# Second FFN of a recurrent decoder step: operands prepared in place and ahead, the last w_out block moved into the phase, the first part's outputs moved later

## The chip, the cores and the metric

The kernel runs on one core of a Trainium2 chip. The metric is device time in microseconds of one execution, and the median of three runs is given. A core has a matrix engine (TensorE, in the profile PE, with its weight loads as PEld), a vector engine (VectorE, DVE), a scalar engine (ScalarE, ACT), GpSimd (POOL) and SyncE (SP), which here issues nearly all DMA transfers, in order.

## The reference

One inference step of a one-layer hybrid decoder over 1104 tokens (16 learned tokens, 64 sample tokens, 1024 prompt tokens) of width 1024:

```
x = x + 0.5 * SwiGLU_1(RMSNorm(x))
x = x + W_out @ concat[RG-LRU, mLSTM, GLA](W_in @ RMSNorm(x))
x = x + 0.5 * SwiGLU_2(RMSNorm(x))
y = RMSNorm(x)                      # the final one
swiglu(x, w1, w3, w2) = (silu(x @ w1) * (x @ w3)) @ w2      # inner width 2816
```

All in float32; the states of the recurrences are outputs too.

## The kernel before

Activations lie transposed, 128 partitions of features by tokens. Every product of two float32 matrices is made of three matmuls in a rounded format: `split(hi, lo, x)` (L106) lets ScalarE cast x into hi, and VectorE subtract hi from x into lo; hi.hi + hi.lo + lo.hi are summed in a PSUM bank.

The program has three stages. The first FFN and the mixing work on three token blocks (336, 384, 384). In the mixing, nine chunks of recurrences are issued with a raised priority, and `w_out((0, 1), out01)` (L1032), the output projection of token blocks 0 and 1, fills TensorE between them. `w_out((2,), out01)` (L1035) follows for block 2: eight weight tiles of 512 KB, 24 matmuls of 384 columns for each, and a residual that is loaded, added and stored (`out01`, L987). The projection's inputs `ys[b]` are tiles named sh and sl in the pool `big`.

The second FFN (from L1267) has pools of its own, which lie where the earlier stages' tiles were. It works on two token parts (`PARTS`, L30): 576 tokens in two halves of 288, then 512 in two halves of 256. For each part `operands` (L1320) calls `norms` (L1291): eight squares on ScalarE, seven adds on POOL, sums over partitions by TensorE, a reciprocal root by eleven small VectorE operations (`rsq`, L110), and a broadcast by TensorE. Then it builds four normalised blocks b11, b12, b21, b22 (features by tokens, halved both ways), takes differences of them, and splits seven operands.

With these, a product of 2x2 blocks takes seven block products where eight would be usual (`seven`, L1388; 84 matmuls). A group f0 (two of 22 slices of 128 inner columns, so eleven groups) runs `seven` for w1 and for w3, the gates (L1490 to L1499), and the product with w2 (L1516 to L1527, called gemm2 here; 96 matmuls in part 0 and 48 wider ones in part 1), whose results VectorE adds into X[i]. The weights' own seven combinations are made by POOL (`weights`, L1360) and split into seven tiles. After the last group of part 0, five output blocks are transposed (`turned`, L1435), normed and stored (`output`, L1442). Part 1 ends with a special tail (L1482, L1500).

The framework orders the instructions of each engine by a priority, which is the order in which the program is written unless `high_priority` raises it, and by an estimate of when each is ready. Each engine then runs its list in order. It waits on a tile's buffer until the last user of that memory is done.

Of the kernel before, what the change touches and what calls it, by code (L numbers as in the profile page):

```python
# [7 lines left out]
F32 = mybir.dt.float32  # L8
# [3 lines left out]
OP = mybir.AluOpType  # L12
# [15 lines left out]
RB = 4  # L28

# [6 lines left out]
def tile_step(ctx, tc, A, O):  # L36
# [6 lines left out]
    wp = front.enter_context(tc.tile_pool(name="wp", bufs=3))  # L43
    mixing = ExitStack()
# [54 lines left out]
    def slot(i):  # L99
        return tuple(big.tile([128, 8, NB[i]], F32R, tag=f"{kind}{i}", name=f"{kind}{i}") for kind in ("sh", "sl"))  # L100
# [9 lines left out]
    def rsq(tp, v, p, n, tag=""):  # L110
        y = tp.tile([128, 4], F32, tag="rsy" + tag, name="rsy", bufs=RB)[:p, :n]
        a = tp.tile([128, 4], F32, tag="rsa" + tag, name="rsa", bufs=RB)[:p, :n]
# [158 lines left out]
    def mix(ph):  # L271
# [763 lines left out]
        w_out((2,), out01)  # L1035


    with ExitStack() as ph:
# [4 lines left out]
        park = [big.tile([128, 8, 384], F32R, tag=tag, name=tag) for tag in ("sl1", "sh2", "sl2")]  # L1043
# [223 lines left out]
    with ExitStack() as ph:  # L1267

        def pool(name, bufs=1, **kw):
            return ph.enter_context(tc.tile_pool(name=name, bufs=bufs, reuse_waits="tile", **kw))  # L1270

        xp, lp, op_, wq, tp = pool("x3"), pool("l3"), pool("o3"), pool("w3"), pool("t3", 2)
        pq, pz = pool("q3", 2, space=PSUM), pool("z3", 2, space=PSUM)
        psum["y"] = psum["s"] = psum["a"] = pz
# [7 lines left out]
        gb = xp.tile([128, 1024], F32, tag="gb", name="gb")  # L1282
        nc.sync.dma_start(gb, A["final_norm_g"].rearrange("(o d) -> o d", o=1).partition_broadcast(128))
        X = [xp.tile([128, 8, 2 * n], F32, tag=f"x{i}", name=f"x{i}") for i, (n, _) in enumerate(PARTS)]
        nc.sync.dma_start(X[0][:, :, 0:320], xdr2[0][:, :, 16:336])
        nc.sync.dma_start(X[0][:, :, 320:576], xdr2[1][:, :, 0:256])
        nc.sync.dma_start(X[1][:, :, 0:128], xdr2[1][:, :, 256:384])
        nc.sync.dma_start(X[1][:, :, 128:512], xdr2[2])


        def norms(i):  # L1291
            n = PARTS[i][0]
            r = tp.tile([128, 2, 288], F32, tag="rb", name="rb", bufs=1)[:, :, :n]
            acc = tp.tile([128, 576], F32, tag="h", name="acc", bufs=3)[:, : 2 * n]
            S.activation(acc, X[i][:, 0, :], AF.Square)
            for k in range(1, 8):
                q = tp.tile([128, 576], F32, tag="h", name="sq", bufs=3)[:, : 2 * n]
                S.activation(q, X[i][:, k, :], AF.Square)
                G.tensor_tensor(acc, acc, q, OP.add)  # L1299
            cs = [(o, min(128, n - o)) for o in range(0, n, 128)]  # L1300
            for h in range(2):
                ss = pz_("ssp")
                for j, (o, m) in enumerate(cs):
                    PE.matmul(ss[:m, j : j + 1], acc[:, h * n + o : h * n + o + m], ones[:, :1], start=True, stop=True)
                v = tp.tile([128, 4], F32, tag="rsv", name="rsv", bufs=RB)[:, : len(cs)]
                V.memset(v, 1.0)
                for j, (o, m) in enumerate(cs):
                    V.tensor_scalar(v[:m, j : j + 1], ss[:m, j : j + 1], 1.0 / D, EPS, OP.mult, OP.add)
                y = rsq(tp, v, 128, len(cs))
                q = pz_("rbp")  # L1310
                for j, (o, m) in enumerate(cs):
                    d = tp.tile([128, 128], F32, tag="dg", name="dg", bufs=3)
                    V.tensor_scalar(d[:m, :m], ident[:m, :m], y[:m, j : j + 1], None, OP.mult)
                    PE.matmul(q[:, o : o + m], ones[:m, :], d[:m, :m], start=True, stop=True)
                S.copy(r[:, h], q[:, :n])
            return r

        def operands(i, gname):  # L1320
            n = PARTS[i][0]
            r = norms(i)
            ops = {}
            for p in ORDER:
# [3 lines left out]
            def temp():  # L1328
                return lp.tile([128, 4, 288], F32, tag="bf", name="bf", bufs=4)[:, :, :n]

            def block(fh, th):
                t = temp()
                for k in range(4):
                    S.mul(t[:, k, :], X[i][:, 4 * fh + k, th * n : th * n + n], vc(gname, 4 * fh + k))
                V.tensor_tensor(t, t, r[:, th, None, :].to_broadcast([128, 4, n]), OP.mult)
                return t

            def minus(x, y, out=None):
                out = temp() if out is None else out
                V.tensor_tensor(out, x, y, OP.subtract)  # L1340
                return out

            b11, b12 = block(0, 0), block(0, 1)
            t1 = minus(b12, b11)
            split(*ops[1], b11)
            b22 = block(1, 1)
            t3 = minus(b22, b12, b12)
            t2 = minus(b22, t1)
            split(*ops[6], t2)
            b21 = block(1, 0)  # L1350
            split(*ops[2], b21)
            for p, t in ((7, t3), (5, t1)):
                split(*ops[p], t)
            split(*ops[4], minus(b21, t2, b21))
            split(*ops[3], b22)
            return ops
# [3 lines left out]
        def weights(w, f):  # L1360
            r = []
            for i in range(2):
                t = wq.tile([128, 4, 256], F32, tag="raw", name="wraw", bufs=3)
# [78 lines left out]
        def output(i, j, o, m, x, add=None):  # L1442
            ss = tp.tile([128, 2], F32, tag="ssf", name="ssf", bufs=RB)[:m]
            v = tp.tile([128, 4], F32, tag="rsv", name="rsv", bufs=RB)[:m, :1]
            for q in range(2):
                xq = x[:m, q * 512 : q * 512 + 512]
                if add:
                    add(q, xq)
                sq = tp.tile([128, 576], F32, tag="h", name="sqf", bufs=3)[:m, :512]
                S.activation(sq, xq, AF.Square, accum_out=ss[:, q : q + 1])  # L1450
                G.tensor_tensor(xq, xq, gb[:m, q * 512 : q * 512 + 512], OP.mult)
# [8 lines left out]
            for q in range(2):  # L1460
                h = slice(q * 512, q * 512 + 512)
                xq = x[:m, h]
                if q == 0:
# [3 lines left out]
                nc.sync.dma_start(dst[:, h], xq)  # L1467

        for i, (n, _) in enumerate(PARTS):
            ops = operands(i, "ffn2_norm_g")  # L1470
            for f0 in range(0, NFB, 2):
                last = f0 + 2 == NFB
                ys_ = {}
# [16 lines left out]
                for g in range(2):  # L1490
# [8 lines left out]
                    hs.append((hh, hl))  # L1499
                if tail:  # L1500
# [15 lines left out]
                for d in range(8):  # L1516
                    wh, wl = (t[:, :, d % 4 * 128 : d % 4 * 128 + 128] for t in u2[d // 4])
                    for o, m in ((0, n), (n, n)) if 2 * n > 512 else ((0, 2 * n),):
                        p = pz_("p2")
                        c = 0  # L1520
                        for g in range(2):
                            hh, hl = (t[:, o : o + m] for t in hs[g])
                            for w, x in ((wh, hh), (wh, hl), (wl, hh)):
                                PE.matmul(p[:, :m], w[:, g, :], x, start=c == 0, stop=c == 5)  # L1524
                                c += 1
                        xs = X[i][:, d, o : o + m]
                        V.scalar_tensor_tensor(xs, p[:, :m], 0.25, xs, OP.mult, OP.add)  # L1527
                if last:
                    for j, (o, m) in enumerate(PARTS[i][1]):
                        x = lp.tile([128, 1152], F32, tag="bf", name="xt", bufs=4)[:, :1024]  # L1530
                        turned(x, i, o, m)
                        output(i, j, o, m, x)
# [52 lines left out]
```

## Time and profile before

| | |
|---|---|
| median of three runs | 2263.55 us (2262.5 to 2268.26) |
| the profiled execution: time, span | 2263.99 us, 2262.2 us |
| mean granted clock of TensorE | 0.968 |
| PE busy, DVE busy, ACT busy, POOL busy | 94%, 68%, 38%, 16% of the span |
| second FFN | from about 1385 us to the end |

The span runs from the first to the last instruction; the time includes what lies around it. A stretch is two times in us from the span's start. The granted clock is a share of full speed: 1.00 is 2.4 GHz and 0.50 is 1.2 GHz. Matmuls overlap, so the time that one adds is found by dividing a stretch by their count.

### The profile page before, as it was taken

The page shows a single profiled execution, that of the slowest core. Times are in us where ns is not written, and L with a number is a line of the kernel's source. Part 1 is how long each engine was busy: PE and PEld are TensorE (multiplying, and loading weights), DVE is VectorE, ACT ScalarE, POOL GpSimd, SP SyncE. Part 2 cuts the span into 40 slices and gives each one's busy share as a digit, 9 for nine tenths or more (in the row PEclk, how much of TensorE's full clock was granted, in tenths as well). Part 3 has the DMA queues.
Part 4 walks back from the last instruction along what each step waited for, and adds up shares of the span by engine and source line. Part 5 has one row for each costly group of instructions (what it writes and reads, how often), then busy time and mean ns, then how long its engine had stood idle before and what let it go on. Part 6 is the DMA issues. An engine that isn't in the chain of part 4 may idle for free.

```text
span 2262.2 us, 35535 instructions
## 1 busy us (share of the span) xinstructions
PE 2118.2 (94%) x13758; PEld 2039.8 (90%) x13758; DVE 1532.1 (68%) x3207; ACT 865.6 (38%) x1701; POOL 371.4 (16%) x345
## 2 busy tenths in 40 slices
PE   8999999999999999999997995699999965999997
PEld 7999999999999999989987895699999955899996
DVE  6544445445444486665877862887888877888886
ACT  6211111111111155546556643443434344444443
POOL 3000000000000040000000002333333322434331
PEclk9999999999999999999998997699999986999999
DMA  5111111111111135434443356132333221333321
GB/s 176 34 51 38 47 38 47 47 38 55 30 56 48 38 112 138 140 115 130 114 123 83 84 149 201 54 94 85 94 94 94 85 74 44 103 94 112 103 94 47
DMA packets 237437, 192.50 MB, mean 85 GB/s; under 512 B 42079, under 2 KB 216708, under 8 KB 237012
## 3 DMA queue, kind: packets, MB, share of 16 engines
q1 hardware_dynamic: 232476, 188.45, 28.3%
q10 hardware_dynamic: 4792, 1.78, 0.4%
q8 instruction: 108, 1.77, 0.3%
q14 instruction: 61, 0.50, 0.1%
HBM read 159.40 MB, written 30.80 MB: 84 GB/s over the span
## 4 chain that ended last, share of the span: by engine, by line
PE 84%; DVE 8%; ACT 3%; DMA 3%; issue 1%; POOL 1%; SPq 0%; ACTq 0%; DVEq 0%; POOLq 0%
PE p L191 23%; PE p L1524 11%; PE p L240 11%; PE b L1397 9%; PE pw L191 8%; PE a L1397 6%; PE c L1397 5%; PE pwo L191 4%; PE pq L545 1%; DVE sl L129 1%; PE pA L747 1%; DVE wlo L108 1%; DVE rsa L116 1%; POOL acc L1299 1%; DVE rsy L118 1%
## 5 line engine op out<-in xcount | busy, mean ns | idle before, releaser
L107 ACT CAST whi<-wraw 128x512 fp32r<-128x512 f32 (+1 forms) x234 | 188.7, 806 | 345.0 <-PE p L240 116.4
L108 DVE TENSOR_TENSOR wlo<-wraw,whi 128x512 fp32r<-128x512 f32 (+1 forms) x234 | 244.7, 1046 | 19.7 <-ACT whi L107 16.9
L242 DVE SCALAR_TENSOR_TENSOR x<-p,x 128x384 f32<-128x384 f32 (+1 forms) x264 | 139.5, 539 | 154.1 <-PE p L240 153.6
L191 PE MATMUL p<-sh,whi 128*128 128x384 f32 (+1 forms) x1056 | 205.3, 332 | 0.4 <-ACT sh L128 0.4
L191 PE MATMUL p<-sl,whi 128*128 128x384 f32 (+1 forms) x1056 | 203.4, 330 | 0.0
L191 PE MATMUL p<-sh,wlo 128*128 128x384 f32 (+1 forms) x1056 | 202.1, 330 | 0.0
L1527 DVE SCALAR_TENSOR_TENSOR x<-p,x 128x288 f32<-128x288 f32 (+1 forms) x256 | 131.6, 526 | 76.2 <-PE p L1524 75.1
L191 PEld LDWEIGHTS p<-sh,whi 128*128 128x128 f32 x1056 | 179.7, 189 | 1.6 <-ACT sh L128 1.4
L191 PEld LDWEIGHTS p<-sh,wlo 128*128 128x128 f32 x1056 | 180.8, 188 | 0.0
L107 ACT CAST hh<-h 128x384 fp32r<-128x384 f32 (+3 forms) x110 | 61.4, 558 | 310.5 <-DVE h L224 278.3
L191 PEld LDWEIGHTS p<-sl,whi 128*128 128x128 f32 x1056 | 179.8, 188 | 0.1
L1372 POOL TENSOR_TENSOR ws<-wraw 128x512 f32<-128x512 f32 x88 | 136.1, 1546 | 258.3 <-DMA wraw<-in_ffn_w_dram 170.5
L240 PE MATMUL p<-hh,whi 128*128 128x384 f32 (+1 forms) x528 | 174.3, 330 | 1.9 <-DVE x L242 1.8
L240 PE MATMUL p<-hh,wlo 128*128 128x384 f32 (+1 forms) x528 | 174.2, 330 | 0.0
L240 PE MATMUL p<-hl,whi 128*128 128x384 f32 (+1 forms) x528 | 173.8, 329 | 0.0
L1397 PE MATMUL b<-op,whi 128*128 128x288 f32 (+1 forms) x1056 | 164.4, 293 | 6.4 <-ACT op L107 3.3
L107 ACT CAST whi<-ws 128x512 fp32r<-128x512 f32 x176 | 108.6, 620 | 160.7 <-PE b L1397 88.7
L1524 PE MATMUL p<-hl,w2h 128*128 128x288 f32 (+1 forms) x512 | 166.2, 326 | 2.2 <-DVE hl L108 2.2
L1524 PE MATMUL p<-hh,w2h 128*128 128x288 f32 (+1 forms) x512 | 163.2, 328 | 4.5 <-DVE x L1527 3.7
L1524 PE MATMUL p<-hh,w2l 128*128 128x288 f32 (+1 forms) x512 | 165.6, 325 | 0.0
L1397 PEld LDWEIGHTS b<-op,whi 128*128 128x128 f32 x1056 | 148.2, 192 | 10.6 <-ACT op L107 4.0
L143 POOL TENSOR_TENSOR acc<-acc,sq 128x384 f32<-128x384 f32 (+1 forms) x21 | 22.8, 1086 | 774.0 <-ACT sq L142 773.5
(455 smaller groups left out, 4619.6 us busy)
## 6 DMA issues: line engine op xcount, KB each, us to landing
wraw<-in_ffn_w_dram SPq DMA_DIRECT2D x154, 512.0 KB
w<-in_ffn_w_dram SPq DMA_DIRECT2D x44, 512.0 KB
wraw<-in_w_in_dram SPq DMA_DIRECT2D x16, 512.0 KB
wraw<-in_w_out_dram SPq DMA_DIRECT2D x16, 512.0 KB
out_y_prompt_dram<-xt SPq DMA_DIRECT2D x16, 256.0 KB
xspill<-x SPq DMA_DIRECT2D x2, 1536.0 KB
stg<-xspill SPq DMA_DIRECT2D x16, 192.0 KB
xspill<-stg SPq DMA_DIRECT2D x16, 192.0 KB
```

Source lines behind the costliest of these rows:

```text
L107: S.copy(hi, x)
L108: V.tensor_tensor(lo, x, hi.bitcast(F32), OP.subtract)
L116: V.tensor_tensor(a, y, y, OP.mult)
L118: V.scalar_tensor_tensor(y, a, 1.5, y, OP.add, OP.mult)
L143: G.tensor_tensor(sums[b], sums[b], s, OP.add)
L191: PE.matmul(p, wsl(ww, k), xsl(xx, k), start=i == 0, stop=i == tot - 1)
L240: PE.matmul(p[:, :n], w[:, g, :], x[:, :n], start=i == 0, stop=i == 3 * GRP - 1)
L242: V.scalar_tensor_tensor(X[b][:, d, :n], p[:, :n], 0.25, X[b][:, d, :n], OP.mult, OP.add)
L1372: G.tensor_tensor(t, x, y, op)
L1397: PE.matmul(t[:, :n], ww[:, k, :], xx[:, k, :], start=first and i == 0, stop=i == 11, skip_group_check=True,)
L1524: PE.matmul(p[:, :m], w[:, g, :], x, start=c == 0, stop=c == 5)
L1527: V.scalar_tensor_tensor(xs, p[:, :m], 0.25, xs, OP.mult, OP.add)
```

## The change

- Tiles sh2 and sl2 (the projection's input for block 2, and the first stage's parking place) move from `big` to a pool `yk` on the other side of the memory, which lives on into the second FFN.
- `w_out((2,))` goes from the end of the mixing to the second FFN as `wout2`, with a priority raised by 400, on weight tiles of the pool there (a fourth raw buffer is added), adding straight into X[1]. The residual for it is loaded from the first spill.
- `norms` adds on VectorE, not on POOL, and takes one root for both halves. `normal` multiplies X[i] in place by gain and root; `differences` and `operands` work on X[i] itself with two temporaries.
- X[0] is loaded again after its operands are split; X[1] is stored to `xback` and loaded again.
- norms(1) stands at group 4 of part 0, normal and differences at group 6; operands(1) in the last group, ahead of its gemm2.
- The outputs of part 0 follow group 2 of part 1, and their gain is multiplied on VectorE together with the root.
- The pool l3 (gates, w2 tiles, the final gain) is opened when `yk` is closed, and so lies on its place.

```diff
-        w_out((2,), out01)
...

+        pool = yk if i == 2 else big
...
-                G.tensor_tensor(acc, acc, q, OP.add)
+                V.tensor_tensor(acc, acc, q, OP.add)
...
+        def normal(i, r, ks):
+            n = PARTS[i][0]
+            for k in ks:
+                x = X[i][:, k, :].rearrange("p (h t) -> p h t", h=2)
+                V.scalar_tensor_tensor(x, x, vc("ffn2_norm_g", k), r, OP.mult, OP.mult)
...
+        def differences(i):
+            b11, b12, b21, b22 = blocks(i)
+            t1, t2 = temp(i), temp(i)
+            minus(t1, b12, b11)
+            minus(t2, b22, t1)
+            minus(b12, b22, b12)
+            return t1, t2
+
+        def operands(i, ts):
+            n = PARTS[i][0]
+            b11, t3, b21, b22 = blocks(i)
+            t1, t2 = ts
             ops = {}
+            for p, x in zip(ORDER, (b11, t2, b21, t3, t1, t2, b22)):
+                if p == 4:
+                    minus(t2, b21, t2)
                 t = op_.tile([128, 2, 4, 288], F32R, tag=f"op{p}", name=f"op{p}")
                 ops[p] = (t[:, 0, :, :n], t[:, 1, :, :n])
+                split(*ops[p], x)
             return ops
...
+        def wout2():
+            wo = A["w_out"].rearrange("(k p) f -> p k f", p=128)
+            for d in range(8):
+                raw = wq.tile([128, 4, 256], F32, tag="raw", name="wraw", bufs=4)
+                raw = raw.rearrange("p k f -> p (k f)").rearrange("p (k f) -> p k f", f=128)
+                nc.sync.dma_start(raw, wo[:, :, d * 128 : d * 128 + 128])
+                u = []
+                for c in range(2):
+                    hi = wq.tile([128, 4, 128], F32R, tag="whi", name="whi", bufs=7)
+                    lo = wq.tile([128, 4, 128], F32R, tag="wlo", name="wlo", bufs=7)
+                    split(hi, lo, raw[:, 4 * c : 4 * c + 4, :])
+                    u.append((hi, lo))
+                p = pz_("pwo")[:, :384]
+                i = 0
+                for a, b in ((0, 0), (0, 1), (1, 0)):
+                    for k in range(8):
+                        PE.matmul(p, u[k // 4][a][:, k % 4, :], ys[2][b][:, k, :], start=i == 0, stop=i == 23)
+                        i += 1
+                x = X[1][:, d, 128:512]
+                V.tensor_tensor(x, x, p, OP.add)
+
+        load0()
+        nc.sync.dma_start(X[1][:, :, 0:128], xdr2[1][:, :, 256:384])
+        nc.sync.dma_start(X[1][:, :, 128:512], xdr[2])
+        normal(0, norms(0), range(8))
+        ts = differences(0)
+        ops = operands(0, ts)
+        load0()
+        with tc.high_priority(offset=W2):
+            wout2()
+        late.close()
+        nc.sync.dma_start(xback, X[1])
+        lp = pool("l3")
...
+                if i == 0 and f0 == 4:
+                    r1 = norms(1)
+                if i == 0 and f0 == 6:
+                    normal(1, r1, range(8))
+                    ts = differences(1)
...
+                if i == 0 and last:
+                    ops = operands(1, ts)
+                    nc.sync.dma_start(X[1], xback)
...
+                gemm2(i, u2, hs)
+                if i == 1 and f0 == 2:
+                    outputs(0)
```

## Rows read from the trace of the kernel before

**Rows 1.** The page: busy time by engine; PE in 40 slices, tenths.

```profile
PE 2118.2 (94%) x13758; PEld 2039.8 (90%) x13758; DVE 1532.1 (68%) x3207; ACT 865.6 (38%) x1701; POOL 371.4 (16%) x345
...
PE   8999999999999999999997995699999965999997
```

**Rows 2.** Stretches: length, then busy time (and instructions) by engine, clock, DMA share, GB/s.

```profile
1385.50:1429.50 44.00, 4.13 (x18) 3.64 (x18) 20.41 (x43) 15.90 (x27) 21.97 (x15) 0.55 0.62 201
...
1429.50:1455.00 25.50, 18.01 (x75) 16.25 (x76) 21.28 (x22) 13.09 (x21) 2.87 (x2) 0.64 0.07 22
...
1455.00:1800.00 345.00, 344.99 (x2604) 344.53 (x2603) 290.98 (x471) 145.89 (x248) 131.65 (x86) 1.00 0.30 90
...
1800.00:1842.50 42.50, 35.76 (x240) 32.30 (x240) 29.63 (x54) 7.99 (x11) 1.28 (x1) 1.00 0.22 70
...
1842.50:1887.00 44.50, 9.71 (x51) 7.79 (x52) 31.61 (x102) 23.70 (x54) 21.45 (x17) 0.59 0.19 65
...
1887.00:1950.00 63.00, 54.78 (x362) 51.52 (x361) 57.81 (x76) 31.83 (x56) 22.23 (x14) 0.85 0.24 67
...
1950.00:2200.00 250.00, 250.00 (x1753) 233.70 (x1752) 214.51 (x324) 113.91 (x194) 94.86 (x65) 1.00 0.33 102
```

**Rows 3.** Waits of SP's queue, 1340 to 1440: total, times, longest.

```profile
SPq L1285 <- PE pwo L191: 2.7, 1, 2.7
```

**Rows 4.** Timeline of SP's issues: start, length, instruction.

```profile
1352.64 0.32 SPq L992 DMA_DIRECT2D xspill<-stg  x1
...
1385.46 0.53 SPq L1285 DMA_DIRECT2D x<-xspill  x1
```

**Rows 5.** Chain of waits through the first hole: start, length, what.

```profile
1348.18 3.39 DMA zg<-z_g
...
1352.75 32.70 PE pwo L191 x187
...
1386.74 8.56 DMA x<-xspill
...
1408.24 1.23 PE ssp L1304 x6
...
1422.29 1.20 DVE dg L1313
...
1429.48 1.37 DVE op L108
```

**Rows 6.** DMA in 1385 to 1400.

```profile
DMA packets 4185, 4.64 MB, mean 309 GB/s; under 512 B 94, under 2 KB 3906, under 8 KB 4185
```

**Rows 7.** Chain of waits through the second hole.

```profile
1870.49 0.72 ACT xt L1464
...
1886.25 1.22 PE a L1397 x4
```

**Rows 8.** VectorE's groups, 1354 to the end: count, busy us, mean ns, idle before.

```profile
L108 DVE TENSOR_TENSOR wlo<-ws,whi 128x512 fp32r<-128x512 f32 x176 | 143.9, 823 | 1.5 <-ACT whi L107 1.3
...
L1404 DVE TENSOR_TENSOR c<-p,b 128x288 f32<-128x288 f32 x66 | 29.5, 447 | 19.5 <-PE b L1397 18.9
...
L1494 DVE SCALAR_TENSOR_TENSOR h<-h,c 128x512 f32<-128x512 f32 x22 | 15.7, 743 | 0.2 <-ACT h L1493 0.2
...
L1340 DVE TENSOR_TENSOR bf<-bf 128x1152 f32<-128x1152 f32 x4 | 5.3, 1347 | 0.0
...
L1340 DVE TENSOR_TENSOR bf<-bf 128x1024 f32<-128x1024 f32 x4 | 4.8, 1218 | 0.0
```

**Rows 9.** Timeline of VectorE, root for half a part.

```profile
1878.55 0.22 DVE L1308 TENSOR_SCALAR rsv<-ssp 128x1 f32<-128x1 f32 x2 [7.51 <-PE ssp L1304]
...
1880.98 0.48 DVE L1313 TENSOR_SCALAR dg<-ident,rsy 128x128 f32<-128x128 f32 x2
```

**Rows 10.** Timeline of PE, eight transposes at the end of the kernel.

```profile
2229.77 1.04 PE L1439 MATMUL xps<-ident,x 128*128 128x128 f32 x8
```

**Rows 11.** Instructions on tile ws, 1500 to 1600: minimum, median, maximum ns.

```profile
L108 DVE TENSOR_TENSOR wlo<-ws,whi x24: 676/684/1476, 1500.5 to 1595.6; 128x512 fp32r<-128x512 f32 x24
```

More of the change, by code (lines that the diff above doesn't have):

```diff
@@ L43, in tile_step @@
     wp = front.enter_context(tc.tile_pool(name="wp", bufs=3))
+    late = ExitStack()
+    yk = late.enter_context(tc.tile_pool(name="yk", bufs=1, side="right"))
     mixing = ExitStack()
@@ L99, in slot @@
     def slot(i):
-        return tuple(big.tile([128, 8, NB[i]], F32R, tag=f"{kind}{i}", name=f"{kind}{i}") for kind in ("sh", "sl"))
+        pool = yk if i == 2 else big
+        return tuple(pool.tile([128, 8, NB[i]], F32R, tag=f"{kind}{i}", name=f"{kind}{i}") for kind in ("sh", "sl"))
     cols, cuts = list(NB), list(CHUNKS)
@@ L1042, in tile_step @@
         X = [xp.tile([128, 8, NB[b]], F32, tag=f"x{b}", name=f"x{b}") for b in range(3)]
-        park = [big.tile([128, 8, 384], F32R, tag=tag, name=tag) for tag in ("sl1", "sh2", "sl2")]
+        park = [p.tile([128, 8, 384], F32R, tag=tag, name=tag) for p, tag in ((big, "sl1"), (yk, "sh2"), (yk, "sl2"))]
         xt = {}
@@ new lines, in norms @@
+            cs = [(h, o, min(128, n - o)) for h in range(2) for o in range(0, n, 128)]
+            ss = pz_("ssp")
+            for j, (h, o, m) in enumerate(cs):
+                PE.matmul(ss[:m, j : j + 1], acc[:, h * n + o : h * n + o + m], ones[:, :1], start=True, stop=True)
+            v = tp.tile([128, 8], F32, tag="rsv", name="rsv", bufs=RB)[:, : len(cs)]
+            if n % 128:
+                V.memset(v, 1.0)
+                for j, (h, o, m) in enumerate(cs):
+                    V.tensor_scalar(v[:m, j : j + 1], ss[:m, j : j + 1], 1.0 / D, EPS, OP.mult, OP.add)
+            else:
+                V.tensor_scalar(v, ss[:, : len(cs)], 1.0 / D, EPS, OP.mult, OP.add)
@@ L1315, in norms @@
+            y = rsq(tp, v, 128, len(cs))
+            for h in range(2):
+                q = pz_("rbp")
+                for j, (hh, o, m) in enumerate(cs):
+                    if hh == h:
+                        d = tp.tile([128, 128], F32, tag="dg", name="dg", bufs=3)
+                        V.tensor_scalar(d[:m, :m], ident[:m, :m], y[:m, j : j + 1], None, OP.mult)
+                        PE.matmul(q[:, o : o + m], ones[:m, :], d[:m, :m], start=True, stop=True)
                 S.copy(r[:, h], q[:, :n])
@@ L1338, in minus @@
[L1338 to L1353, printed above, removed]
@@ L1442, in output @@
         def output(i, j, o, m, x, add=None):
+            ahead = add is not None
             ss = tp.tile([128, 2], F32, tag="ssf", name="ssf", bufs=RB)[:m]
-            v = tp.tile([128, 4], F32, tag="rsv", name="rsv", bufs=RB)[:m, :1]
+            v = tp.tile([128, 8], F32, tag="rsv", name="rsv", bufs=RB)[:m, :1]
             for q in range(2):
@@ L1462, in output @@
                 xq = x[:m, h]
-                if q == 0:
+                if not ahead:
+                    V.scalar_tensor_tensor(xq, xq, r, gb[:m, h], OP.mult, OP.mult)
+                elif q == 0:
                     S.mul(xq, xq, r)
@@ new lines, in tile_step @@
+        load0()
[10 more added lines that the diff above has]
+        lp = pool("l3")
+        gb = lp.tile([128, 1024], F32, tag="gb", name="gb")
+        nc.sync.dma_start(gb, A["final_norm_g"].rearrange("(o d) -> o d", o=1).partition_broadcast(128))
@@ new lines, in gemm2 @@
+        def gemm2(i, u2, hs):
+            n = PARTS[i][0]
+            for d in range(8):
+                wh, wl = (t[:, :, d % 4 * 128 : d % 4 * 128 + 128] for t in u2[d // 4])
+                for o, m in ((0, n), (n, n)) if 2 * n > 512 else ((0, 2 * n),):
+                    p = pz_("p2")
+                    c = 0
+                    for g in range(2):
+                        hh, hl = (t[:, o : o + m] for t in hs[g])
+                        for w, x in ((wh, hh), (wh, hl), (wl, hh)):
+                            PE.matmul(p[:, :m], w[:, g, :], x, start=c == 0, stop=c == 5)
+                            c += 1
+                    xs = X[i][:, d, o : o + m]
+                    V.scalar_tensor_tensor(xs, p[:, :m], 0.25, xs, OP.mult, OP.add)
@@ L1515, in tile_step @@
                     break
[L1516 to L1532, printed above, removed]
+                gemm2(i, u2, hs)
+                if i == 1 and f0 == 2:
+                    outputs(0)
 _INS = [
```

61 lines of the change are left out of this document (22 added, 39 removed).

## The prediction

> **What bounds the kernel now.** The page's head and its slices come first [rows 1]: TensorE (PE) is busy for 94% of the span, VectorE for 68%, and the PE slices drop below nine tenths in a shallow dip past the middle and in two deeper ones after it. So the kernel is TensorE-bound except in these two holes (the shallow dip, in the mixing, is not touched), and the change is about these. The table of stretches [rows 2] gives their size. Between the holes, from 1455 to 1800 us, 2604 matmuls take 345.0 us, 0.1325 us each, with TensorE never idle, the clock at its upper level (2.4 GHz) and VectorE at 84%. From 1950 to 2200 it is 1753 in 250.0 us, 0.1426 each, VectorE at 86%.
>
> The first hole: the last w_out block ends at 1385.4. By 1455 only 75 matmuls of the second FFN have been issued, which at 0.1325 is 9.9 us of work, so its first part runs as if it had started at 1445.1. Lost: 59.7 us. The second hole: in 1800 to 1842.5 there are 240 matmuls, 31.8 us of work, so 10.7 are lost. Then come 44.5 us with nearly none, and 362 matmuls from 1887 to 1950, 51.6 us of work at the later rate, so part 1 runs as if it had started at 1898.4; 55.9 lost. Together 66.6 us. In both holes the granted clock is 0.55 to 0.64, that is mostly the lower level (1.2 GHz); these counts contain that.
>
> Why the first hole is there is read from the chain of waits [rows 5] (the list names one step of each kind): w_out block (32.7 us of matmuls), load of X[0], eight squares and POOL adds, the sums over partitions, the reciprocal root, the diagonal, then one block at a time to the first split operand, which ends at 1430.9. The load itself waits for the last w_out matmul [rows 3] because X[0] lies where sh2 and sl2 were. Its data were there much earlier: the last store of token blocks 0 and 1 was issued at 1352.64, the load at 1385.46 [rows 4]. The second hole is the same chain, behind the five output blocks of part 0, which end at 1871.2; the first product of part 1 is at 1886.3 [rows 7].
>
> **The change, first hole.** It takes sh2 and sl2 off X[0]'s place, so the load can go at about 1352.6, 33 us earlier, and puts the w_out block on TensorE meanwhile. Step by step:
>
> The load was issued at 1385.46 and the first square started at 1395.33, after a stretch at 309 GB/s [rows 6]: 9.9 us. Now the eight w_out weight tiles (512 KB each) come on the same queue, and X[1] too. I add 3.5 us, for one such tile and a half ahead of it at that rate: squares start at 1366. Bounds are 0, if the scheduler puts X[0] first, and 14, if all eight tiles come first (4.2 MB at 309 GB/s).
>
> The w_out block now needs weight tiles of its own pool, which lie where the mixing's tiles were, so its first tile can't be fetched ahead. A small load in the chain is 3.4 us [rows 5] and a split of 128x512 is 0.7 on VectorE after a cast of about the same; I take 4.5 us later, ending at 1390. Bounds 0 and 8. Each of its eight products is 4.1 us of TensorE, over 2 splits and 1 add on VectorE, 1.9 us.
>
> Squares and adds: POOL's steps took from 1396.7 to 1408.2. On VectorE a two-input pass of 128x512 is 0.74 us where little disturbs it [rows 8]; for 128x576 I take 0.8. Seven of them and a square ahead are 6 us: 1372. Sums to diagonal took 14.1 us (1408.24 to 1422.29 [rows 5]), and 2.4 us for the same arithmetic with nothing between (1878.55 to 1880.98 [rows 9]); I take 7 with the sums' matmuls, since w_out's splits hold 1.9 of each 4.1 us: 1379. Broadcast and copies: 3.5. Eight in-place products of 0.8 and three differences of 1.35 [rows 8] are 10, and 13 with the rest of the w_out splits; cast and split of operand 1 are 2.5. First product: 1398.
>
> There TensorE is paced by VectorE for seven products: 7 operand splits of 1.35, 7 weight splits of 0.68 [rows 11] and 5 evictions of 0.45 [rows 8] are 16.5 us against 84 x 0.1325 = 11.1, so 5 lost, and I allow 2 for the lower clock after a gap of 8 us. Part 0 then runs as if started at 1405. **Saved in the first hole: 1445 - 1405 = 40 us.** Bounds: it can't start before the w_out block's end plus the 5, so at most 51; with the load 10 later still (its bound of 14), the w_out block 3.5 later and weights for the first products another 14 late behind all that, 12.
>
> The second load of X[0] waits on SP's queue for the last operand split, at about 1412, and the xback store for the last w_out add. Behind them on SP are the w2 tiles and the second weight set. The first FFN eviction that needs X[0] comes after two sets of 84 products, 22 us after the first; the reload is 2.36 MB, 7.6 us at 309 GB/s. I cost it at nothing, hidden by those products; without that cover it is 8 us, which lies inside those 14. The l3 tiles lie on sh2's place and so wait for the w_out block; it ends before the first product, so nothing.
>
> **The change, second hole.** What goes: the whole norm and block chain between the parts, and the output blocks, leave the hole. What stays at the seam: seven operand casts and splits (7 passes of 128x1024 at 1.2 us on VectorE [rows 8]), released one by one as the last products of part 0 free their tiles, beside the last gates (six passes, 4.4), 16 evictions of 0.45, the w2 splits (2.4) and seven weight splits of 0.68. All that is 27 us of VectorE against the gemm2 work left, which was 31.8 us in the trace [rows 2]. So it nearly hides; I leave 8 of the 66.6 us. If the gemm2 work is no longer left over there, the seam costs 15; if it hides fully, 0.
>
> What is added to the busy stretches. TensorE: 40 transposes of 0.13 us (eight in 1.04 us, [rows 10]) and eight small matmuls, 7 us with their PSUM turns. VectorE in part 0: 15 two-input passes of 128x512 (0.70), three differences of 1.2 and a root of 2.9: 17 us. In part 1: five blocks of two products (0.72) and 13 tiny operations (0.16): 18 us. The stretches have 15% of VectorE free, 5.3 us in each group of 35 us. The 17 fall on two groups and the 18 on about two, so 6 and 8 exceed what is free; weights are split one set ahead, and I charge half: 8 us with rounding up. POOL's adds and gain products of the first part go away and cost nothing, as POOL waits most of the time.
>
> Left in the second hole: 8 + 7 + 8 = 23. **Saved: 66.6 - 23 = 43.6.**
>
> Here a row and a rule meet. The same weight split of 128x512 takes 676 ns at least, 684 in the median and 1476 at most [rows 11], and 823 in the mean over the whole FFN [rows 8]; POOL's own passes run beside it. The Trainium skill, "SBUF — State Buffer", section "Who interferes with whom", says that a VectorE instruction with two SBUF inputs and a GpSimd instruction that reads SBUF exclude each other for the whole instruction, and so speaks against moving adds off POOL into a stretch where POOL still works. The spread of that row agrees. By the rule each moved pass costs its mean and not its minimum, and the sum would be that of the first rival below, 2216; by the median it is 2180.
>
> **Sum.** 2263.99 us (the profiled execution; its span is 2262.2) - 40 - 43.6 = 2180.4. The median of the runs shown is 0.4 lower, so 2180.
>
> **The rivals.**
> VectorE becomes the bound: its idle time in the busy stretches is waiting in step with TensorE and can't be used, so all moved work delays TensorE one for one: 17 + 18 + 8.4 us, times 823/684 = 52, and 7 of TensorE. The second hole then gives back 66.6 - 59 = 8. 2264 - 40 - 8 = 2216. For it: 84 to 86% in every stretch. Against it: TensorE never idled there. 14%.
>
> The w_out block hides nothing: X[0], the weights of w_out and those of the first products queue on one ring, and the first products start late. First hole 12 instead of 40: 2208. For it: 0.62 of all DMA time was already used there [rows 2]. 12%.
>
> Both hide better than I allow: 51 and 58: 2155. 8%.
>
> The preparation of part 1 doesn't run ahead: norms(1) needs tiles of the three "h" buffers that the gates use too, and slips to the seam; the 16 us from 1871 to 1887 stay: 2196. 5%.
>
> On the other side: the late outputs hold TensorE. Each block's transposes need one of two "bf" tiles, which comes free only when the store of the block before last has landed, and TensorE works in order. The five blocks took 29 us, 1842 to 1871, with all engines free for them. It costs more than the gain of 84 only from 17 us of held TensorE per block, three times that. 5%: 2% near no change, 3% slower, about 2290.
>
> The likeliest, 56%, is 2180, its own range 2166 to 2196. The range that leaves out no more than 2 in 10 takes in the two costly rivals: 2156 to 2216. A difference under 0.3% (7 us) can't be told from none here. Faster 0.95, same 0.02, slower 0.03.
>
> **What would show it.** First hole: the load of X[0] issued before the last w_out matmuls; no granted clock under 0.8 in a 25 us stretch from 1385 on; the first product near 1398. Second hole: no stretch of 25 us under 20 us of TensorE between the parts; the five output blocks spread inside part 1. VectorE at 0.9 over the second FFN. It would be wrong if TensorE showed new waits on weight splits in the groups that carry the moved work, on X[0]'s reload at the first evictions, or on transposes.

## The result and the profile after

The changed kernel takes 2229.08 us in the median (2227.4 to 2232.74, 4 runs) against 2263.03 for the kernel before, measured beside it: a ratio of 0.9848, 95% interval 0.9828 to 0.9868. It is faster by 34 us where 84 were forecast, and 13 us slower than the upper end of the range. The direction was right, the size was not.

The page of the changed kernel, its lines for TensorE, to be read beside [rows 1]: the matmuls are the same in number, and the shallow dip of the mixing is still there. The first deep hole (slices of 5 and 6) is now one slice of 4, further forward; of the second, two dents of 8 are left.

```profile
PE 2110.8 (95%) x13758; PEld 2035.0 (91%) x13758; DVE 1535.4 (69%) x3214; ACT 848.7 (38%) x1672; POOL 330.6 (15%) x321
...
PE   8999999999999999999998894999999989889997
```

The table of stretches, with the columns of [rows 2]:

```profile
1349.60:1386.40 36.80, 5.83 (x25) 5.05 (x24) 14.50 (x40) 9.67 (x16) 0.00 (x0) 0.56 0.80 226
1386.40:1425.00 38.60, 36.28 (x204) 35.54 (x204) 35.80 (x41) 18.06 (x25) 8.61 (x6) 0.97 0.51 168
1425.00:1775.00 350.00, 338.53 (x2525) 335.99 (x2525) 299.60 (x481) 146.09 (x252) 124.08 (x86) 1.00 0.31 96
1775.00:1850.00 75.00, 67.66 (x506) 66.95 (x505) 65.59 (x102) 32.25 (x51) 25.77 (x15) 0.93 0.34 111
1850.00:1925.00 75.00, 71.63 (x520) 68.34 (x520) 58.24 (x94) 29.49 (x51) 22.06 (x17) 0.98 0.29 92
1925.00:1975.00 50.00, 34.68 (x201) 29.96 (x200) 37.44 (x108) 23.58 (x51) 6.19 (x5) 0.83 0.27 90
1975.00:2180.00 205.00, 204.65 (x1431) 190.93 (x1430) 183.70 (x270) 91.16 (x157) 72.27 (x50) 1.00 0.30 96
```

Three things are to be seen. There is still a hole of 37 us, now ahead of the w_out block (clock 0.56). The body of part 0, where TensorE lost nothing before, now loses: 2525 matmuls in 350 us. And the five late output blocks leave a dent at 1925 to 1975.

By 1500 us the products of the second FFN count 564 in the changed kernel (450 with w1 and w3, 114 of gemm2) and 405 in the one before (345 and 60; rows below). At the 0.1325 us of one, part 0 runs as if started at 1425.3 against 1446.3: **21 us came from the first hole, where 40 were forecast.** The profiled executions differ by 35.3 us (2263.99 and 2228.67), so **14.3 came from the second, where 43.6 were forecast**: of its 66.6 us, 52.3 are still lost somewhere, not 23. Such splits by count hold to some 3 us: the w_out block begins at 1386.45 here, and at 1384.10 and 1383.17 in two runs below that differ from this kernel only behind it.

Products with w1 and w3 and of gemm2 from 1350 on, in the changed kernel and then in the one before (stretch, TensorE's time and count, clock, DMA share, GB/s):

```profile
1350.00:1500.00 150.00, 62.43 (x450) 0.89 0.54 166
...
1350.00:1500.00 150.00, 17.89 (x114) 0.89 0.54 166
```

```profile
1350.00:1500.00 150.00, 54.77 (x345) 0.81 0.39 122
...
1350.00:1500.00 150.00, 8.93 (x60) 0.81 0.39 122
```

### The profile page after: what moved, and what is told of

It is laid out like the page before. It is cut to its first block, busy times and chain, and to the rows that moved or that the text cites. A ratio compares the mean times of both kernels' runs of the same rounds, so it can differ in the third digit from the quotient of the medians.

```text
span 2226.9 us, 35462 instructions
## 1 busy us (share of the span) xinstructions
PE 2110.8 (95%) x13758; PEld 2035.0 (91%) x13758; DVE 1535.4 (69%) x3214; ACT 848.7 (38%) x1672; POOL 330.6 (15%) x321
## 4 chain that ended last, share of the span: by engine, by line
PE 83%; DVE 9%; ACT 3%; DMA 2%; issue 2%; SPq 1%; DVEq 0%; ACTq 0%
PE p L196 24%; PE p L245 11%; PE p L1528 10%; PE pw L196 10%; PE b L1405 8%; PE c L1405 5%; PE a L1405 5%; PE pwo L196 2%; DVE wlo L113 1%; PE pq L550 1%; PE pwo L1498 1%; PE pA L752 1%; DVE sl L134 1%; PE pgt L464 0%; DVE hl L113 0%
## 5 line engine op out<-in xcount | busy, mean ns | idle before, releaser
L113 DVE TENSOR_TENSOR wlo<-ws,whi 128x512 fp32r<-128x512 f32 x176 | 136.5, 779 | 5.2 <-ACT whi L112 4.1
```

Of the source, the lines that this page charges most:

```text
L113: V.tensor_tensor(lo, x, hi.bitcast(F32), OP.subtract)
```

## Experiments on the first hole

TensorE's longest wait of the changed kernel between 1345 and 1450 (total, times, longest), and its timeline there (start, length, instruction, and in brackets the wait before it and what ended it):

```profile
PE ssp L1307 <- DVE acc L1303: 27.9, 1, 27.9
```

```profile
1377.61 2.31 PE L1307 MATMUL ssp<-ones,acc 128*128 128x1 f32 x12 [27.86 <-DVE acc L1303]
1383.02 3.50 PE L1322 MATMUL rbp<-dg,ones 128*128 128x128 f32 x12 [3.10 <-DVE dg L1321]
1386.45 2.58 PE L1498 MATMUL pwo<-sh,whi 128*128 128x384 f32 x8
...
1411.14 1.22 PE L1405 MATMUL a<-op,whi 128*128 128x288 f32 x8
...
1423.30 1.55 PE L1498 MATMUL pwo<-sh,wlo 128*128 128x384 f32 x8
```

ScalarE cast the first w_out weights at 1361.81 (row below), so the first product could have run near 1363. It stood behind the norm's sums, which waited 27.9 us for the squares.

```profile
1361.81 1.14 ACT L112 CAST whi<-wraw 128x512 fp32r<-128x512 f32 x2 [12.26 <-DMA wraw<-in_w_out_dram]
```

What holds that order? Not the priority: with W2 at 2500 instead of 400 the instruction lists of all engines come out identical. The sums (ssp), the broadcasts (rbp) and the w_out products (pwo) share two PSUM banks, which are handed out in the order of the text, and there the norm stands first.

**Own banks for w_out.**

```diff
-                p = pz_("pwo")[:, :384]
+                p = bank("ac"[d % 2])[:, :384]
```

> The eight w_out products take their PSUM tile from two of the six banks of the products a and c, which nothing uses yet, instead of the two banks that they shared with the norm's sums (ssp) and broadcasts (rbp). Theory 1 (the shared banks): in the changed kernel the first w_out product has to take its bank after rbp, so it stood behind the whole norm on TensorE though its first weights were split by 1363.7. With banks of its own the block starts near 1364 and ends near 1400, and the sums stand behind it; the chain from sums to first operand (root, eight products, differences, splits: about 20 us) then starts at 1400, so the first product comes near 1420 instead of 1411 and the part starts as if at 1420 instead of 1424: 0 to 8 us faster, 2221 to 2229, with the hole not gone but moved behind the block. Rival (loads): X[0], X[1] and the w_out weights come late on one ring, whatever the order; the block then still starts after 1380 and the time stays within 3 us of 2229.

Measured 2223.63 (ratio 0.9821, 95% interval 0.9806 to 0.9835, which overlaps that of the changed kernel a little). Its timeline:

```profile
1359.69 2.93 PE L1498 MATMUL a<-sh,whi 128*128 128x384 f32 x8 [12.87 <-ACT whi L112]
...
1394.10 1.55 PE L1498 MATMUL c<-sh,wlo 128*128 128x384 f32 x8
1395.49 1.34 PE L1307 MATMUL ssp<-ones,acc 128*128 128x1 f32 x12
...
1408.87 1.33 PE L1405 MATMUL a<-op,whi 128*128 128x288 f32 x4 [4.71 <-ACT op L112]
```

One line moved the whole block 27 us forward, so the shared banks were the cause and the loads were not. But the sums now wait behind the block, and part 0 runs as if started at 1417.7 (621 products by 1500).

**The norm between the products.** Two ways: the block cut by hand into three pieces, still on the shared banks (first; the third piece stands behind the norm), and own banks with the norm at a higher priority (second).

```diff
+            if i == 0:
+                wout2(range(0, 3))
             ss = pz_("ssp")
...
             y = rsq(tp, v, 128, len(cs))
+            if i == 0:
+                wout2(range(3, 5))
...
+        wout2(range(5, 8))
...
-        with tc.high_priority(offset=W2):
-            wout2()
```

> The w_out block is written in three pieces inside the norm of part 0: three products ahead of the sums over partitions, two ahead of the broadcasts, three behind. Theory 1 (the shared banks and TensorE's order set by them): products run while ACT and VectorE do the squares and the root, the block ends near 1400, the first product of the FFN near 1405; effective start 1405 to 1410 instead of 1424, 14 to 19 us faster: 2210 to 2215. Rival (loads late): the pieces wait for weights, not for banks; under 5 us, 2224 to 2229. Rival (VectorE): the w_out splits and adds go in front of the norm's adds on VectorE, and the norm's end is as late as before: 5 to 10 us.

```diff
-        normal(0, norms(0), range(8))
+        with tc.high_priority(offset=2500):
+            r0 = norms(0)
+        normal(0, r0, range(8))
```

> As the kernel with own banks for the w_out products, and the norm of part 0 written with a higher priority, so that TensorE's list has the sums after the fifth product and the broadcasts after the seventh, with everything else in the same order. Theory 1 (TensorE's order, set by the shared banks): in the run with own banks the sums stood ready at 1378.6 and waited until 1395.5 behind the block; now the root and the products run beside the last three w_out products, the block ends near 1398 and the first product follows at once, near 1400 instead of 1409: 7 to 12 us faster than that run, 2211 to 2217. Rival (VectorE is what counts from 1395 on: in that run it was busy for 23 of 25 us from 1400 and for 25 of 25 from 1425): the operand splits and the first weight splits fill it whenever they start, and only 1 to 4 us are won, 2219 to 2223.

The first took 2234.32 (0.9871, 0.9854 to 0.9887), no gain over the changed kernel: without the priority the w_out loads stand behind those of X[0] and X[1], and TensorE waited 20.9 us for its first weights, until 1368.63. The second took 2220.07 (0.9811, 0.9793 to 0.9828), which the intervals do not tell from own banks alone. There the sums ran at 1383, the broadcasts at 1394 and 1398, and the first product came at 1403.86, 5 us earlier; yet by 1500 it has 619 products and starts as if at 1418.0. The table of stretches says why (the columns are those of [rows 2]):

```profile
1400.00:1450.00 50.00, 38.14 (x252) 35.75 (x251) 50.00 (x57) 25.67 (x40) 32.76 (x10) 0.90 0.52 174
```

VectorE is busy for 50.00 of 50 us: eight products, differences, seven operand splits and the first weight sets fill it whenever they start. The rival that named VectorE from 1395 on had the better forecast. Not all of these 50 us are work, though: from 1424.85 on, ten of VectorE's passes took 0.6 to 1.1 us longer than others of their shape, some 9 us together, while POOL's own passes ran (rows in the last section).

## Experiments on the second hole

**Leaving the two moved parts out.** One kernel drops the call of outputs(0). The other drops norms(1), normal(1) and differences(1) and sets the two temporaries to zero.

> Leaves out the five output blocks of part 0 (their rows of the output are not written). Measures what the late outputs cost. Theory (late outputs hold TensorE for about as long as in the hole that they left): 15 to 22 us faster, 2207 to 2214. Rival (they are hidden, TensorE pays the 40 transposes alone): 5 to 8 us faster, 2221 to 2224, and the waits at 1936 to 1959 turn up as something else.

> Leaves out the sums, the normalising products and the differences of part 1 (part 1 then runs on tokens that are not normalised, with zeros for two of its operands). Measures what the work ahead costs inside part 0. Theory (VectorE pays one for one in lost TensorE time): the 17.6 us that part 0 lost between 1425 and 1775 come back, 14 to 20 us faster, 2209 to 2215. Rival (the order of VectorE's list and its bursts, whatever work is in it: a wait of 2.3 us on an eviction at 1600 is after all of that work): under 8 us faster, 2221 to 2229.

Measured 2205.97 (0.9739, 0.9724 to 0.9753) and 2205.41 (0.9740, 0.9726 to 0.9755): the late outputs cost 23.1 us, the work ahead for part 1 costs 23.7, each give or take a few us. If the two add, about 5.5 of the 52.3 us are left for the seam itself, where 8 were forecast.

The stretch 1525 to 1775, in the changed kernel, then without the work ahead, then with that work paced (next run):

```profile
1525.00:1775.00 250.00, 239.75 (x1784) 237.69 (x1783) 207.14 (x341) 98.89 (x169) 79.21 (x57) 0.99 0.28 86
```

```profile
1525.00:1775.00 250.00, 250.00 (x1890) 249.80 (x1890) 214.74 (x340) 108.35 (x182) 83.55 (x58) 1.00 0.31 91
```

```profile
1525.00:1775.00 250.00, 245.59 (x1844) 243.95 (x1844) 216.55 (x355) 104.60 (x178) 81.47 (x58) 1.00 0.30 89
```

106 matmuls, 14.0 us, are lost to the work ahead in this stretch. But VectorE is *busier* in the kernel that loses nothing (214.74) than in the one that does (207.14): its total is not the bound. Nor is the loss where the passes are. In the changed kernel VectorE's products for part 1 run from 1552.6 to 1559 and the three differences end at 1568.6, but the 25 us from 1550 lose 8 matmuls, and later ones 30 and 20 (changed kernel; without the work ahead these three have 191, 190 and 191):

```profile
1550.00:1575.00 25.00, 24.44 (x183) 23.97 (x182) 25.00 (x34) 9.18 (x17) 9.38 (x7) 1.00 0.18 55
...
1600.00:1625.00 25.00, 22.68 (x160) 22.44 (x159) 19.16 (x33) 7.14 (x12) 6.26 (x5) 0.93 0.24 78
...
1700.00:1725.00 25.00, 22.89 (x171) 22.46 (x170) 19.46 (x34) 9.14 (x16) 7.64 (x5) 1.00 0.29 85
```

**Pacing the products.** In VectorE's list the eight products stand in one run (one and seven). Written into four groups they still come out in one run, since they are ready; so each pair is made to wait for its group's result. The differences follow the last pair, at group 14.

```diff
+                if pace:
+                    V.scalar_tensor_tensor(r1[:, :, 0:1], t[1][:, 0:2].rearrange(...), 0.0, r1[:, :, 0:1], OP.mult, OP.add)
+                    normal(1, r1, range(f0 - 6, f0 - 4))
```

> The same work ahead for part 1, but its eight products go two by two into four groups: each pair is made to wait for the group's first-FFN result (a product with zero of one column is added to the factors, one tiny operation per pair). Leaving the work out won 24 us, 14 of them between 1525 and 1775. Theory 2 (bursts: eight passes in a row stand ahead of evictions in VectorE's list, not the sum of the work; VectorE was 0.83 busy there, and 0.86 without any loss in the run without the work): half of the 14 or more comes back, 2217 to 2224. Rival (the sum of the work, one for one): 2226 to 2232.

Measured 2222.62 (0.9821, 0.9804 to 0.9838, overlapping that of the changed kernel a little): 6.5 us back in the medians, and 60 of the 106 matmuls, 8.0 us, in that stretch, with more passes than before. So more than half of the loss there came from the products' standing in one run and from where they stood, not from their sum. The waits of the changed kernel from 1560 to 1775 are for evictions that came late, nearly all of them after the last of these passes; how the run makes later evictions late is not shown:

```profile
PE b L1405 <- DVE c L1412: 5.0, 4, 2.1
PE p L1528 <- DVE x L1531: 2.3, 1, 2.3
PE c L1405 <- DVE c L1412: 1.7, 1, 1.7
```

The 2.3 us are followed by a lower clock, 0.93 in the slice of 25 us: single matmuls start 0.24 us apart instead of 0.13.

```profile
1600.10 0.29 PE L1528 MATMUL p<-hh,w2l 128*128 128x288 f32 x1
1602.72 0.40 PE L1528 MATMUL p<-hh,w2h 128*128 128x288 f32 x1 [2.32 <-DVE x L1531]
...
1603.66 0.45 PE L1528 MATMUL p<-hh,w2h 128*128 128x288 f32 x1
1603.90 0.45 PE L1528 MATMUL p<-hl,w2h 128*128 128x288 f32 x1
```

**The adds of part 1 back on POOL** (`(V if i == 0 else G).tensor_tensor(acc, acc, q, OP.add)`).

> The seven adds of part 1's sum of squares go back to POOL; seven passes of 0.7 us less on VectorE. Theory 2 (bursts; the adds stood one by one between other work in VectorE's list): 0 to 3 us faster, 2226 to 2229. Rival (the sum of the work, one for one, 24 us for about 20 of passes): 5 to 7 us faster, 2222 to 2224. Rival (the passes of POOL slow those of VectorE): slower than 2229.

Measured 2226.50 (0.9842, 0.9822 to 0.9863). The interval is nearly that of the changed kernel: whether seven passes less on VectorE are worth nothing or their sum of 4.8 us (seven of 0.68) can't be told from it.

**The output blocks: one to a group, one to every second group, back where they were, and with a third tile.**

```diff
-                if i == 1 and f0 == 2:
-                    outputs(0)
+                if i == 1 and 2 <= f0 <= 10:                    # one to a group
+                    outputs(0, [f0 // 2 - 1])
+                if i == 1 and f0 % 4 == 2 and f0 <= 18:         # every second group
+                    outputs(0, [f0 // 4])
+                if i == 0 and last:                             # back
+                    outputs(0)
...
-        ... pool("t3", 2), pool("b3", 2)
+        ... pool("t3", 2), pool("b3", 3)                        # third tile
```

> The five output blocks of part 0 one in each of five groups of part 1 instead of all behind the second group. In the changed kernel TensorE's list has all 40 transposes in one row, 8 and 32, and without the blocks the kernel took 23 us less. Theory 3 (TensorE is held because the blocks queue for two tiles, two PSUM banks and the stores among themselves): spread, only the 5 us of transposes and a little clock remain, 12 to 18 us faster, 2211 to 2217. Rival (each block costs its 4 to 5 us wherever it stands, by its work on VectorE): within 4 us of 2229.

> The five output blocks one in every second group of part 1. One to a group won 9.6 of the 23 us that they cost; 5.2 are transposes. Theory 3b (each block costs its own share wherever it stands, by its work on ACT and VectorE and by its transposes): as one to a group, 2217 to 2221. Rival (two blocks in neighbouring groups still meet at the tiles and the stores): 4 us or more faster than one to a group, 2215 or less.

> The output blocks of part 0 go back to where they were, right behind part 0, with all else as changed. In the kernel before they took 29 us there, with TensorE idle; now the operands of part 1 are ready and its products can run beside them. If the late place saved what the prediction took (their time in the hole, 29 us, against 7 of transposes and a part of 18 of VectorE): 10 us or more slower than 2229. Theory 3 (what costs is that all 40 transposes stand in one row of TensorE's list, wherever): within 5 us of 2229.

> A third tile for the output rows of the first part (and for the two differences). In the changed kernel the third output block copied its transposes only when the first block's store had landed: TensorE waited 5.5 us there, and 7.3 us more for ACT at the end of the five blocks. Theory 3a (the two tiles and the store): the first wait goes, 4 to 7 us faster, 2222 to 2225. Rival (ACT and VectorE in order: the copies queue behind the squares and the roots of the block before): the time moves to the next wait, under 3 us.

Measured: one to a group 2219.47 (0.9807, 0.9791 to 0.9824), every second group 2217.03 (0.9799, 0.9782 to 0.9815), back behind part 0 2225.81 (0.9828, 0.9812 to 0.9844), third tile 2225.30 (0.9833, 0.9818 to 0.9847). No gain of the late place is seen: with the operands of part 1 ready the blocks cost no more right behind part 0. In both kernels all 40 transposes stand in one row of TensorE's list. The changed kernel's waits from 1925 to 1975, and two rows of its timeline:

```profile
PE xps L1447 <- ACT xt L1448: 7.7, 4, 5.5
PE a L1405 <- ACT c L1420: 7.3, 1, 7.3
```

```profile
1946.57 1.07 ACT L1448 COPY xt<-xps 128x512 f32<-128x512 f32 x2 [4.79 <-DMA out_y_sample_dram<-xt]
1947.21 1.97 PE L1447 MATMUL xps<-ident,x 128*128 128x128 f32 x8 [5.47 <-ACT xt L1448]
```

Its chain of waits there names the store:

```profile
1944.11 2.31 DMA out_y_sample_dram<-xt
```

The third block's copy waits for the first block's store, since there are two tiles, and TensorE waits behind the copy. The store itself is 2.31 of these 4.79 us; the rest is the first block's root and products on VectorE (until 1944), and the fifth copy waits 3.57 us more, put down to a root on VectorE. ScalarE runs its list in order, so the eviction that TensorE waited 7.3 us for stands behind that copy. With a third tile the first wait is shorter, 3.00 us, and the eviction is still waited for, 5.9 us; spread, one 3.6 us wait on ACT is the longest left there, and about half of the 23.1 us comes back. The rest holds 5 us of transposes; what the other 6 are was not separated.

With a third tile (timeline), and in every second group (waits from 1850 to 1975):

```profile
1943.83 1.97 PE L1447 MATMUL xps<-ident,x 128*128 128x128 f32 x8 [3.00 <-ACT xt L1448]
```

```profile
PE a L1405 <- ACT c L1420: 3.6, 1, 3.6
```

## Experiments on the edits together

> The three edits together: own banks for the w_out products with the norm of part 0 ahead in priority (9 us alone), the products of part 1 paced over four groups (6.5 alone), the output blocks one to a group (9.6 alone). Theory (three separate losses at three places): they add to 25 us, 2200 to 2208. Rival (one shared loss, VectorE's total: what is freed at one place is waited for at the next): under 18 us, 2211 or more.

> The three edits together, and four passes more off VectorE where it was busy all the time: one of the three differences of part 0 (128x1152) and the residues of three of the seven operands of part 1 (128x1024) go to POOL. Theory (at these two places, 1400 to 1450 and 1773 to 1793, VectorE is the bound): 5 us of its passes go, 2 to 5 us faster than the three edits alone. Rival (POOL's own passes there slow VectorE's, or are late for the products that need them): no gain, or slower than the three edits alone.

The passes that go to POOL:

```diff
-            minus(b12, b22, b12)
+            minus(b12, b22, b12, V if i else G)
...
+                if i and p in (5, 4, 3):
+                    hi, lo = ops[p]
+                    S.copy(hi, x)
+                    G.tensor_tensor(lo, x, hi.bitcast(F32), OP.subtract)
```

> The three edits together with a third tile for the output rows. If the blocks spread over the groups no longer meet at the tiles: as the three edits together, 2206 to 2210. If the store still holds a block: 2 to 5 us less, 2203 to 2206.

> The three edits together, with the seven adds of part 1 on POOL (2.5 us alone) and the output blocks in every second group. If the small gains add: 2203 to 2207. If VectorE is no longer what is waited for between 1450 and 1775 once the products are paced: 2207 to 2210.

| edits | us, median | ratio to before, 95% |
|---|---|---|
| three together | 2208.65 | 0.9750 (0.9734 to 0.9766) |
| and passes on POOL | 2212.04 | 0.9767 (0.9752 to 0.9781) |
| three and a third tile | 2207.81 | 0.9758 (0.9743 to 0.9772) |
| three, adds on POOL, every second group | 2202.76 | 0.9736 (0.9722 to 0.9751) |

The three give 20.4 of the 25 us that they gave alone; 2208.65 lies between the two forecasts, nearer to separate losses at separate places. The last version is the fastest complete one, 60 us below the kernel before and 26 below the changed one. The passes moved to POOL did not help: ScalarE waited 10.0 us for the difference on POOL, and TensorE 8.4 us for weights. ScalarE's waits in that kernel, 1400 to 1430:

```profile
ACT op L112 <- POOL x L1340: 10.0, 1, 10.0
```

## Why the prediction was wrong, step by step

**"Puts the w_out block on TensorE meanwhile", "ending at 1390": failed.** The block began at 1386.45 and ended at 1424.9. I costed its loads and splits but not the place of the norm's 24 small matmuls in TensorE's list, nor the two banks that fix it. Own banks took it back to 1359.69 to 1395.7 and won 7.6 us by the count of products (5.5 in the medians). In the changed kernel part 0 starts as if at 1425.3, right at the block's end, so the late block is the whole of the 20 us missing there. The rival "hides nothing" priced the first hole at 12 saved instead of 40, where 21 were; but it gave the loads as the cause, and that is refuted.

**"Squares start at 1366": 1370.24**, a small miss. Four w_out tiles were issued ahead of X[0]'s second half, not one and a half (3.5 us at 309 GB/s are two tiles; one and a half are 2.5); SP's rows:

```profile
1352.38 9.23 SPq L1487 DMA_DIRECT2D wraw<-in_w_out_dram  x4
1361.71 1.69 SPq L1292 DMA_DIRECT2D x<-xspill  x1
```

The chain behind the squares came out in sum: in the changed kernel the first operand was split by 1396.05 (VectorE's row below), where 1398 was forecast. That is in part luck, as the w_out splits that the sum put between its steps mostly came later; and TensorE was in the w_out block by then.

```profile
1394.70 1.35 DVE L113 TENSOR_TENSOR op<-x,op 128x1152 fp32r<-128x1152 f32 x1
```

**"First product: 1398", then "5 lost" and "2 for the lower clock": failed in size.** With order and banks put right the first product is at 1403.86 and part 0 starts as if at 1418.0: 14 lost, not 7. I counted operand splits, weight splits and evictions of seven products; VectorE also has the rest of the differences, w2 splits and the second weight set, and is full for 50 us, some 9 of them passes stretched beside POOL's. The bound of at most 51 saved does not come out of its terms either: 1445.1 less 1390 and 5 is 50, and with the block at its old end 55.

**"The 17 fall on two groups", "I charge half": failed.** The work ahead cost 23.7 us. The charge took the share of VectorE that is free in a stretch for time that added passes can use. The first rival (VectorE one for one) has a price near the measured one, 17 x 823/684 = 20, but its reason does not hold in the body: VectorE did more there without any loss. Shown is that pacing the products gives back 8.0 of the 14.0 us lost from 1525 to 1775. Why TensorE waits after 1575, when no pass of that work is left, is open; an order fixed ahead for a TensorE that ran earlier would do it, but no run tested this.

**"40 transposes", "7 us with their PSUM turns", and a part of 8 for VectorE: failed in size, 23.1.** The losing rival "the late outputs hold TensorE" had the mechanism, two tiles and a store, with the root on VectorE ahead of the store; its price was 4.6 us a block, not 17. The prediction credited the late place with what the ready operands do: back behind part 0 the blocks cost no more.

**The seam: 8 forecast**, about 5.5 by subtraction. **Reload of X[0] and the xback store "at nothing": right**; no wait of TensorE names them.

**The range**, 2156 to 2216, took in either costly rival alone. Here both holes fell short at once, by 19 and 29 us, which makes the 48 between 2180 and the profiled 2228.67; the prediction gave the two together no chance of their own.

**What would show it.** The load did go ahead of the w_out products, and no 25 us of the seam had under 20 us of TensorE (20.08 from 1775 to 1800). The clock from 1385 to 1410 was 0.93, since the low clock came earlier (0.59 from 1350 to 1375); it fell again to 0.76 from 1950 to 1975. The first product near 1398, VectorE at 0.9 (it was 0.85 from 1425 to 2180) and output blocks spread inside part 1 did not hold, and the warning sign was there: new waits of TensorE on transposes, and, in place of weight splits, on evictions behind the moved work.

## What to carry to other kernels

Work that is to hide a chain hides it only if it stands ahead of the chain's own instructions in the engine's list: look for small matmuls of the chain on the same engine, and for PSUM tiles that are handed out in the order of the text. What added passes cost an engine that is busy for 85% is not read from that share: here some 17 us of them cost 23.7. It can matter whether they stand one at a time or in one run in that engine's list; tying each pair to a group gave back 8.0 us in one stretch. Before crediting a later place, ask whether what made the old place dear is removed by another part of the same change.

## What the runs showed of the hardware

A pass on POOL can be starved. In the run with the norm ahead, one 128x512 combination of weights took 18.33 us on POOL, where others take 1.3 to 2.4; VectorE had no gap in that time. But VectorE was just as full from 1425 to 1450 (25.00 of 25), and POOL's passes ran. What differs is the kind of VectorE's passes. From 1406.52 to 1424.48 every one of them has two inputs in SBUF; POOL's pass ended at 1425.71, just after the first one with an input from PSUM (VectorE's first row below), and the split behind that took 1.42 us instead of 0.69. POOL spans are rough, but in the run with passes on POOL another engine bears it out: the 10.0 us that ScalarE waited, behind a pass of 9.70. That one ended at 1419.46, after VectorE had run out of work at 1418.34. Timelines of POOL and of VectorE with the norm ahead:

```profile
1397.48 1.29 POOL L1380 TENSOR_TENSOR ws<-wraw 128x512 f32<-128x512 f32 x1 [1.17 <-DVE wlo L113]
1407.38 18.33 POOL L1380 TENSOR_TENSOR ws<-wraw,ws 128x512 f32<-128x512 f32 x1 [8.61 <-DVE wlo L113]
1425.79 1.62 POOL L1380 TENSOR_TENSOR ws<-wraw 128x512 f32<-128x512 f32 x1
```

```profile
1424.48 0.46 DVE L1412 TENSOR_TENSOR c<-p,b 128x288 f32<-128x288 f32 x1
1424.85 1.42 DVE L113 TENSOR_TENSOR wlo<-ws,whi 128x512 fp32r<-128x512 f32 x1
```

The Trainium skill, "SBUF — State Buffer", section "Who interferes with whom", has it that a VectorE instruction with two SBUF inputs and a GpSimd instruction that reads SBUF block each other for a whole instruction, whichever starts first. The trace agrees that one of them blocks; it adds that POOL stayed behind many such VectorE instructions in a row, not one.

The queue of SP took 9.23 us to issue four w_out loads of 512 KB, 2.3 us each, while the DMA engines were full (share 1.12 from 1350 to 1375). The kernel before issued such loads from 1287 to 1345 in 0.38 to 0.42 us each. So behind other loads in a full stretch a load is issued late as well; whether the issue or the full engines set the time was not separated.
